# Joining the recurrence's diagonal with its last level, and asking for head norms before applying them, in a two-block kernel on one core

## The chip, the cores and the metric

The kernel runs on one core of a Trainium2 chip. The metric is the device time of one execution in microseconds (us); the median of three runs before the change is 1014.35 us (1013.6 to 1016.02).

## The reference, cut to what matters

The reference applies a first block (two layers) and a second block (two layers) to 256 tokens of 1024 channels, all in float32. The parts that the change touches are the first block's recurrence, its head norms, and a head norm in the second block's odd mixer:

```
# recurrence (per head, chunks of 64 tokens): A is lower triangular, its diagonal has decay 1
decay = exp(where(causal, b[t] - b[s], -inf))
A = einsum('bhtd,bhsd,bhtsd->bhts', qi, ki, decay)
o = einsum('bhts,bhsv->bhtv', A, vi) + einsum('bhtd,bhdv->bhtv', qi * exp(b), S)
o_hg = rmsnorm(o_hg, hgrn_onorm_g[i])
qn  = rmsnorm(heads(nq, 8), nsa_qnorm_g[i])             # 8 query heads of 64
k_sl = partial_rope(rmsnorm(heads(ksl, 2), ...), cos, sin)   # and k_wn: key heads of 64
gv = rmsnorm_2(g.reshape(..., 8, 64), g_norm)           # odd mixer, gate heads
```

## The kernel before

The 256 tokens are two halves of 128, called H = 0 and H = 1, and nearly every step is done once for each. Weights stream from memory in tiles `raw` of 128x1024; ScalarE rounds each to `whi` and VectorE subtracts to get the rest `wlo`; a projection multiplies whi by x, wlo by x and whi by the rest of x (`mm3`). The pools are small: three raw tiles, five whi and wlo, eight PSUM banks of which `pM`, `pB` and `pC` are single, `pA` two and `acc` three.

The order on each engine is made by a scheduler from the program: it takes the instructions by program order and readiness and gives buffers out as they come free, so a product of a later projection is put between dependent steps. Each engine then runs its own list in that order; an instruction that waits holds up those behind it.

The steps of a first-block layer that matter here, in program order: the key projections `K1` (PSUM `K`, 512 columns, of which the last 256 are four key heads); the projection `hi`; `hkT`, the transposed keys of the recurrence; `ph`, the first products of the compression; `hgrn` for both halves; the query projection `nq` (PSUM `Q`) and `k2` (PSUM `K`, 280 columns); the sparse attention `nsa` (`as`, `apt`, `no`); the gates `hz`, `hgo`, `nz`; and the output product `po`.

`head_rstd` (L528) squares on ScalarE (`sq`), sums on VectorE (`hss`), scales (`hv`), takes the power on GpSimd (`hr`, L412), and, where a row factor f is given, multiplies by f on VectorE (L541). For the keys and the queries it is called inside the loop over halves, right before its result is used (`kn`, `qn`).

`hgrn` (L923) builds the transposed matrix `AT` of a half. At its start four products `pd` of kT and q give every entry, and a copy under a mask of the diagonal (L936) keeps the diagonal. Then seven levels: level lv takes the decays `E`, multiplies keys and queries into them, makes four products `pl` of 128x64 and copies them into AT under that level's mask (L975). The last level, lv 6, has blocks of one token. At the end AT is multiplied with `vh` into `ho`; for H = 1 a product `ptop` and its copy `stop` carry the first half's state.

```
pd = ps_("pd", "pM")
V.copy_predicated(AT[H], lmask_d..., pd...)                       # L936, diagonal
tt(Xv[:, :, :, 0, :], Xv[:, :, :, 0, :], kv[:, :, :, 0, :], OP.mult)   # keys into E
mm(p[:, n * 64:(n + 1) * 64], X[:, n, :], Xv[:, n, :, 1, :])
V.copy_predicated(dst, lmask[:, lv]..., p...)                     # L975, one level
```

Of the kernel before, what the change touches and what calls it, by code (L numbers as in the profile page):

```python
# [14 lines left out]
AF = mybir.ActivationFunctionType  # L15
# [208 lines left out]
def body(ctx: ExitStack, tc: tile.TileContext, a: dict, offs: dict, out: bass.AP):  # L224
# [40 lines left out]
    def tt(o, x, y, op):  # L265
        V.tensor_tensor(o, x, y, op=op)  # L266
# [262 lines left out]
    def head_rstd(ps, nh, width, scale, bias, tag="t2", st="sm", f=None):  # L529

        sq = s2("sq", tag=tag)
        n = nh * width
        act(sq[:, :n], ps, AF.Square, scale=1.0 if f is None else f)
        ss = small("hss", nh, st)
        V.tensor_reduce(ss, sq[:, :n].rearrange("p (h d) -> p h d", h=nh), axis=AX, op=OP.add)
        v = small("hv", nh, st)
        V.tensor_scalar(v, ss, scale, bias, op0=OP.mult, op1=OP.add)
        r = small("hr", nh, st)
        rpow(r, v)
        if f is not None:  # L540
            V.tensor_scalar(r, r, f, None, op0=OP.mult)  # L541
        return r


# [44 lines left out]
    def first_layer(l, nx, nxt, whf=None, lb=None, between=None, whq=None, then=lambda: None):  # L589
# [82 lines left out]
        if l == 0:  # L672
            logs()
        kns = []
        for H in range(2):
            ps = pj[H]
            pk = ps[:, 256:]
            r = head_rstd(pk, 4, 64, 1.0 / 64, EPS, f=rs[H][0])
            kn = s1("kn", tag="t2")
            tt(v3(kn, 4), v3(pk, 4), bc(r, 64), OP.mult)  # L680

            kd = s2("kd", tag="t2").rearrange("p (b g a c) -> p b g a c", b=2, g=2, a=2)
            kn4 = kn.rearrange("p (b g c) -> p b g c", b=2, g=2)
            for a_ in range(2):
                tt(kd[:, :, :, a_, :], kn4, kg[:, 64:].rearrange("p (b c) -> p b c", b=2).unsqueeze(2).to_broadcast([P, 2, 2, 64]), OP.mult)
            kd8 = kd.rearrange("p b g a c -> p (b g a) c")
            rope_heads(kd8, kd8, 8, H)
            kns.append(kd.rearrange("p b g a c -> p b g (a c)"))
# [28 lines left out]
        for H in range(2):  # L717
            o = hgrn(H, lfs[H], ks[H], qT, vh, Ktop)
            r = head_rstd(o, 4, P, 16.0 / P, 16 * EPS, "pr", "sh")
            tt(v3(ys[H], 4), v3(o, 4), bc(r, P), OP.mult)  # L720


        qnT = s4("qnT").rearrange("p (j t) -> p j t", j=4)
# [6 lines left out]
        w = win("k2")  # L730
        vs, gs = [], []
        pj = proj_both(x, w, "K2", "pA")
        for H in range(2):
            ps = pq[H]
            r = head_rstd(ps, 8, 64, 1.0, 64 * EPS, f=rs[H][0])
            qn = s2("qn")
            tt(v3(qn), v3(ps), bc(r, 64), OP.mult)
            tt(v3(qn), v3(qn), bm(qg, 8), OP.mult)
            qr = s2("qr")
            act(qr, qn, AF.Copy)  # L740
            rope_heads(v3(qr), v3(qn), 8, H)
            sl = slice(H * P, (H + 1) * P)
            pt = ps_("qT", "pB")
            for j in range(4):
                PE.transpose(pt[:, j * P:(j + 1) * P], qn[:, j * P:(j + 1) * P], ident)
            V.tensor_copy(qnT[:, :, sl], pt.rearrange("p (j t) -> p j t", j=4))
            q2 = s4("q2", F32R).rearrange("p (n a c) -> p n a c", n=8, a=2)
            act(q2[:, :, 0, :], v3(qr), AF.Copy)
            tt(q2[:, :, 1, :], v3(qr), q2[:, :, 0, :], OP.subtract)
            q2 = q2.rearrange("p n a c -> p n (a c)").bitcast(F32)  # L750
            qs.append(s4("qs", F32R).rearrange("p (n t) -> p n t", n=8))
            for n0 in (0, 4):
                pt = ps_("qT", "pB")
                for n in range(4):
                    PE.transpose(pt[:, n * P:(n + 1) * P], q2[:, n0 + n, :], ident)
                p3 = pt.rearrange("p (n t) -> p n t", n=4)
                if n0:
                    V.tensor_copy(qs[H][:, n0:n0 + 4], p3)
                else:
                    act(qs[H][:, n0:n0 + 4], p3, AF.Copy)  # L760
# [163 lines left out]
    def hgrn(H, lf, kT, qT, vh, Ktop):  # L924


        lv0 = H
        near, off = slice((1 - H) * 64, (2 - H) * 64), slice(H * 64, (H + 1) * 64)
        K3 = Ktop.rearrange("p (h t) -> p h t", h=4)
        kT = kT.rearrange("p (h t) -> p h t", h=4)  # L930
        q = qT[:, :, H * P:(H + 1) * P]

        pd = ps_("pd", "pM")
        for n in range(4):
            mm(pd[:, n * P:(n + 1) * P], kT[:, n, :], q[:, n, :])
        V.copy_predicated(AT[H], lmask_d.rearrange("p (h t) -> p h t", h=4), pd.rearrange("p (h t) -> p h t", h=4))  # L936
        o = ps_("ho", "pC")
        far = small("far", 4, "sf")
        pl = tops = None
        for e4 in range(2):  # L940
            E = wk.tile([P, 4, 4, P], F32, tag="w8", name="E4", bufs=BUFS["w8"])
            for n in range(4):
                ps = ps_("D", "pA")
                for b in range(2):
                    r = (9 * b + 1 - H + 4 * e4) * 64
                    mm(ps[:, b * 256:(b + 1) * 256], lf[b][:, n * P:(n + 1) * P], lev[:, r:r + 256])
                act(E[:, :, n, :].rearrange("p v (b t) -> p b v t", b=2), ps.rearrange("p (b v t) -> p b v t", b=2, v=4), AF.Exp)
            if e4 == 0:

                V.tensor_copy(far.unsqueeze(2), E[:, 0, :, (127, 63)[H]:(128, 64)[H]])  # L950
            for e in range(4 * e4, 4 * e4 + 4):
                lv = e - lv0
                if not 0 <= lv < 7:
                    continue
                w = 64 >> lv
                X = E[:, e % 4, :, :]
                Xv = X.rearrange("p h (b u m) -> p h b u m", u=2, m=w)
                kv = kT.rearrange("p h (b u m) -> p h b u m", u=2, m=w)
                qv = q.rearrange("p h (b u m) -> p h b u m", u=2, m=w)
                tt(Xv[:, :, :, 0, :], Xv[:, :, :, 0, :], kv[:, :, :, 0, :], OP.mult)  # L960
                tt(Xv[:, :, :, 1, :], Xv[:, :, :, 1, :], qv[:, :, :, 1, :], OP.mult)
                if lv == 0:


                    if H:
                        tops = E[:, 0]
                        tt(tops[:, :, near], tops[:, :, near], q[:, :, near], OP.mult)
                    tt((tops if H else K3)[:, :, off], X[:, :, off], bc(far, 64), OP.mult)
                if lv % 2 == 0:
                    pl = ps_("pl", ("pM", "pB")[lv // 2 % 2])  # L970
                p = pl[:, lv % 2 * 256:(lv % 2 + 1) * 256]
                for n in range(4):
                    mm(p[:, n * 64:(n + 1) * 64], X[:, n, :], Xv[:, n, :, 1, :])
                dst = AT[H].rearrange("p h (b u m) -> p (h b) u m", u=2, m=w)[:, :, 1, :]
                V.copy_predicated(dst, lmask[:, lv].rearrange("p h (b m) -> p (h b) m", m=w),  # L975
                                  p.rearrange("p (b m) -> p b m", m=w))
        if H == 0:
            tt(K3[:, :, near], E[:, 3, :, near], kT[:, :, near], OP.mult)
            for n in range(4):
                mm(o[:, n * P:(n + 1) * P], AT[0][:, n, :], vh[0][:, n * P:(n + 1) * P])  # L980
        else:
            px = ps_("ptop", "pM")
            for n in range(4):
                mm(px[:, n * P:(n + 1) * P], Ktop[:, n * P:(n + 1) * P], tops[:, n, :])
            st = s2("stop", tag="pts")
            V.tensor_copy(st, px)
            for n in range(4):
                sl = slice(n * P, (n + 1) * P)
                mm(o[:, sl], AT[1][:, n, :], vh[1][:, sl], True, False)
                mm(o[:, sl], st[:, sl], vh[0][:, sl], False, True)  # L990
        return o
# [193 lines left out]
    def odd_layer(nx, nxt):  # L1185
# [88 lines left out]
                bass.AP(tensor=sap.tensor, offset=sap.offset + par * P, ap=[[0, 64], [2 * P, 4], [1, P]]))  # L1274
        w = win("g")
        pj = proj_both(x, w, "og")
        ms = []
        for H in range(2):
            g = s2("og", tag="gate")
            act(g, pj[H], AF.Gelu_apprx_tanh, scale=rs[H][0])  # L1280
            r = head_rstd(g, 8, 64, 1.0 / 64, EPS)
            tt(v3(g), v3(g), bc(r, 64), OP.mult)
            tt(g, g, sg, OP.mult)
            pm = ps_("pm", "pB")
            for n in range(8):
                mm(pm[n % 2 * 64:n % 2 * 64 + 64, n // 2 * P:(n // 2 + 1) * P], g[:, n * 64:(n + 1) * 64], ws[:, n, :])
            m = s2("mx", tag="nz")
            tt(m, pm, sb, OP.add)
            ms.append(m.rearrange("p (j t) -> p j t", j=4))
# [190 lines left out]
```

## Time and profile before

| | |
|---|---|
| median of 3 runs | 1014.35 us |
| the profiled execution | 1014.08 us |
| its span | 1012.3 us |
| TensorE busy (PE) | 982.1 us, 97% |
| VectorE busy (DVE) | 824.9 us, 81% |
| ScalarE busy (ACT) | 624.0 us, 62% |
| GpSimd busy (POOL) | 45.7 us, 5% |
| granted TensorE clock | 0.9 or more of full speed in every fortieth of the span |

The span runs from the first to the last instruction. Matmuls overlap and their ends are modelled, so PE's busy share says that PE is hardly ever without work, not that it works at its peak; the start of one matmul to the start of the next is the better measure of what one costs. A float32 product shows as two records, one for each of its two weight loads. In a row of the timeline the bracket is the idle time of that engine just before the row and what ended it.

### The profile page before, as it was taken

To read this page: it belongs to the slowest core of one execution; us is meant where nothing else is said; L and a number is where in the kernel's file an instruction comes from. 1 tells how busy PE (TensorE), PEld (TensorE's weight loads), DVE (VectorE), ACT (ScalarE), POOL (GpSimd) and SP (SyncE) were. 2 spreads that over 40 slices of the span, in tenths; PEclk is the share of its full clock that TensorE was granted. 3 is DMA by queue.
4 is the path that set the end of the run, shared out by engine and by line. 5 is a ranking of instruction groups with operands and counts; after the bars stand their busy time and mean duration, and the time that the engine had idled before them with its cause. 6 is when DMAs were issued, how large, how long until landed. Compare 5 with 4: busy or idle time off the path is not lost.

```text
span 1012.3 us, 16208 instructions
## 1 busy us (share of the span) xinstructions
PE 982.1 (97%) x6009; PEld 841.3 (83%) x6009; DVE 824.9 (81%) x1482; ACT 624.0 (62%) x1128; POOL 45.7 (5%) x52
## 2 busy tenths in 40 slices
PE   9999999999998999999999999999999999999997
PEld 6889786788797876799889888888898889888885
DVE  5878899878788898779879988888677889888886
ACT  7753565577644664666657666666756457666664
POOL 1001100000002000000111000000000020000000
PEclk9999999999999999999999999999999999999999
DMA  8832533664504526555754766666572546766661
GB/s 320 304 104 74 181 114 109 215 194 137 182 11 129 164 63 184 170 158 165 231 185 132 223 195 189 191 192 181 167 226 66 169 127 198 215 187 188 187 188 62
DMA packets 49103, 169.02 MB, mean 167 GB/s; under 512 B 5760, under 2 KB 7040, under 8 KB 48384
## 3 DMA queue, kind: packets, MB, share of 16 engines
q1 hardware_dynamic: 48448, 167.17, 54.1%
q8 instruction: 47, 0.77, 0.3%
q10 hardware_dynamic: 576, 0.82, 0.2%
q14 instruction: 32, 0.26, 0.1%
HBM read 165.34 MB, written 1.05 MB: 164 GB/s over the span
## 4 chain that ended last, share of the span: by engine, by line
PE 64%; DVE 9%; ACT 4%; DMA 4%; issue 2%; POOL 1%; POOLq 0%; ACTq 0%; DVEq 0%; SPq 0%
PE up L365 25%; PE pd L365 11%; PE po L365 5%; PE pg L365 3%; DVE wlo L266 3%; PE oq L365 2%; ACT whi L263 2%; PE as L365 1%; PE xT L431 1%; PE xa L365 1%; PE pl L365 1%; PE nz L365 1%; PE hgo L365 1%; PE og L365 1%; PE Q L365 1%
## 5 line engine op out<-in xcount | busy, mean ns | idle before, releaser
L266 DVE TENSOR_TENSOR wlo<-raw,whi 128x1024 fp32r<-128x1024 f32 (+2 forms) x297 | 358.6, 1211 | 86.7 <-ACT whi L263 86.1
L263 ACT ACTIVATE whi<-raw 128x1024 fp32r<-128x1024 f32 (+2 forms) x297 | 309.6, 1045 | 164.8 <-DMA raw<-in_win_dram 17.8
L365 PE MATMUL up<-xN,whi 128*128 128x512 f32 x512 | 180.8, 397 | 0.0
L365 PE MATMUL up<-xN,wlo 128*128 128x256 f32 x512 | 133.3, 281 | 0.0
L365 PE MATMUL pd<-whi,fhl 128*128 128x512 f32 x352 | 115.4, 391 | 0.1
L365 PEld LDWEIGHTS up<-xN,whi 128*128 128x128 f32 x512 | 94.1, 188 | 18.6
L365 PEld LDWEIGHTS up<-xN,wlo 128*128 128x128 f32 x512 | 96.6, 189 | 5.7
L1073 DVE SCALAR_TENSOR_TENSOR fc<-fp,colp,fc 128x255 f32<-128x255 f32 (+1 forms) x176 | 81.5, 479 | 3.0 <-ACT fc L263 0.7
L365 PEld LDWEIGHTS pd<-whi,fhl 128*128 128x128 f32 x352 | 66.0, 188 | 13.0 <-ACT fhl L263 0.5
L365 PE MATMUL pd<-wlo,fhl 128*128 128x512 f32 x176 | 68.6, 390 | 0.0
L263 ACT ACTIVATE upl<-up 128x256 f32<-128x256 f32 x64 | 24.5, 383 | 59.4 <-PE up L365 59.3
L263 ACT ACTIVATE fc<-fp,colp 128x256 f32<-128x256 f32 x88 | 51.0, 590 | 3.9 <-DVE fp L266 3.8
L365 PE MATMUL po<-whi,yA 128*128 128x512 f32 x128 | 41.5, 399 | 2.4 <-ACT yA L263 1.3
L263 ACT ACTIVATE pr<-as,anm 128x128 f32<-128x128 f32 (+1 forms) x80 | 32.5, 422 | 17.8 <-PE apt L1056 6.8
L365 PE MATMUL pg<-whi,xB 128*128 128x512 f32 x128 | 40.6, 393 | 0.0
L365 PEld LDWEIGHTS pd<-wlo,fhl 128*128 128x128 f32 x176 | 33.1, 188 | 6.9
L365 PE MATMUL up<-xD,whi 128*128 128x256 f32 x192 | 35.2, 284 | 0.9 <-DVE xD L436 0.6
L365 PE MATMUL up<-xF,whi 128*128 128x256 f32 x192 | 35.2, 284 | 0.9 <-DVE xF L436 0.6
L266 DVE TENSOR_TENSOR fp<-up,upl 128x256 f32<-128x256 f32 x64 | 27.0, 421 | 10.7 <-ACT upl L263 10.5
L365 PE MATMUL K<-whi,xA 128*128 128x280 f32 (+1 forms) x128 | 33.8, 345 | 0.0
L263 ACT ACTIVATE jk<-h 128x512 f32<-128x512 f32 x36 | 22.7, 637 | 17.4 <-DVE h L266 17.4
L412 POOL TENSOR_TENSOR r<-v,mh 128x2 f32<-128x2 f32 (+1 forms) x10 | 6.7, 672 | 582.0 <-DVE v L472 196.5
(397 smaller groups left out, 2272.6 us busy)
## 6 DMA issues: line engine op xcount, KB each, us to landing
raw<-in_up_dram SPq DMA_DIRECT2D x88, 512.0 KB, 3.6
raw<-in_win_dram SPq DMA_DIRECT2D x62, 512.0 KB, 4.3
raw<-in_down_dram SPq DMA_DIRECT2D x44, 512.0 KB, 3.7
raw<-in_ein_dram SPq DMA_DIRECT2D x20, 512.0 KB, 4.0
raw<-in_oin_dram SPq DMA_DIRECT2D x20, 512.0 KB, 3.8
raw<-in_wout_dram SPq DMA_DIRECT2D x16, 512.0 KB, 3.7
raw<-in_wpg_dram SPq DMA_DIRECT2D x16, 512.0 KB, 4.0
cw<-in_cw_dram SPq DMA_DIRECT2D x4, 1024.0 KB, 7.8
```

What stands on the lines that cost most here:

```text
L263: A.activation(o, i, f, **kw)
L266: V.tensor_tensor(o, x, y, op=op)
L365: PE.matmul(o, l, r, start=start, stop=stop)
L412: G.tensor_tensor(o, v, mh[:, :v.shape[1]], op=OP.pow)
L431: PE.transpose(ps[:, j * P:(j + 1) * P], hc[:, j * P:(j + 1) * P], ident)
L1073: V.scalar_tensor_tensor(dst[:, k:], src[:, :T - k], w, dst[:, k:], op0=OP.mult, op1=OP.add)
```

## The change

It has three parts. First, `head_rstd` no longer multiplies by f; its callers give f to a `scalar_tensor_tensor` that applies f and the norm to the data at once. Second, the norms of both halves are asked for (square, sum, power) ahead of the loop that applies them: for the keys (K1), the queries (nq) and the gate of the odd mixer (og); and the second half's `y` from the recurrence's norm is applied inside the query loop. Third, in `hgrn` the four products `pd` at the start and their copy are gone. At the last level q is copied by ScalarE beside the decayed queries, and one product of 256 columns per head, with kT itself as weights, gives the diagonal (z = 0) and the last level (z = 1); the decay of the last level's even tokens is 1, so the keys need no multiplication. The results lie in banks pB and pM, two heads each, and go to AT by two masked copies per bank: 256 columns under the diagonal's mask and the 128 odd ones under the level's.

```diff
@@ head_rstd
         rpow(r, v)
-        if f is not None:
-            V.tensor_scalar(r, r, f, None, op0=OP.mult)
         return r
@@ first_layer, K1
+        krs = [head_rstd(pj[H][:, 256:], 4, 64, 1.0 / 64, EPS, f=rs[H][0]) for H in range(2)]
         for H in range(2):
-            ps = pj[H]
-            pk = ps[:, 256:]
-            r = head_rstd(pk, 4, 64, 1.0 / 64, EPS, f=rs[H][0])
+            pk = pj[H][:, 256:]
             kn = s1("kn", tag="t2")
-            tt(v3(kn, 4), v3(pk, 4), bc(r, 64), OP.mult)
+            V.scalar_tensor_tensor(v3(kn, 4), v3(pk, 4), rs[H][0], bc(krs[H], 64), op0=OP.mult, op1=OP.mult)
@@ first_layer, after hgrn
-            tt(v3(ys[H], 4), v3(o, 4), bc(r, P), OP.mult)
+            if H == 0:
+                tt(v3(ys[H], 4), v3(o, 4), bc(r, P), OP.mult)
@@ first_layer, queries
+        qrs = [head_rstd(pq[H], 8, 64, 1.0, 64 * EPS, f=rs[H][0]) for H in range(2)]
         for H in range(2):
-            ps = pq[H]
-            r = head_rstd(ps, 8, 64, 1.0, 64 * EPS, f=rs[H][0])
             qn = s2("qn")
-            tt(v3(qn), v3(ps), bc(r, 64), OP.mult)
+            V.scalar_tensor_tensor(v3(qn), v3(pq[H]), rs[H][0], bc(qrs[H], 64), op0=OP.mult, op1=OP.mult)
             tt(v3(qn), v3(qn), bm(qg, 8), OP.mult)
+            if H == 0:
+                tt(v3(ys[1], 4), v3(o, 4), bc(r, P), OP.mult)
@@ hgrn
-        pd = ps_("pd", "pM")
-        for n in range(4):
-            mm(pd[:, n * P:(n + 1) * P], kT[:, n, :], q[:, n, :])
-        V.copy_predicated(AT[H], lmask_d.rearrange("p (h t) -> p h t", h=4), pd.rearrange("p (h t) -> p h t", h=4))
@@ hgrn, level loop
+                tt(Xv[:, :, :, 1, :], Xv[:, :, :, 1, :], qv[:, :, :, 1, :], OP.mult)
+                if lv == 6:
+                    z = E[:, 0, :, :]
+                    act(z, q, AF.Copy)
+                    for i in range(2):
+                        pl = ps_("pl", ("pB", "pM")[i]).rearrange("p (n z t) -> p n z t", n=2, z=2)
+                        for n in range(2):
+                            mm(pl[:, n], kT[:, 2 * i + n, :], E[:, 0:e % 4 + 1:e % 4, 2 * i + n, :])
+                        hs = slice(2 * i, 2 * i + 2)
+                        dst = AT[H][:, hs]
+                        V.copy_predicated(dst, lmask_d.rearrange("p (h t) -> p h t", h=4)[:, hs], pl[:, :, 0])
+                        odd = lambda t: t.rearrange("p h (b u) -> p h b u", u=2)[:, :, :, 1]
+                        V.copy_predicated(odd(dst), lmask[:, lv, hs], odd(pl[:, :, 1]))
+                    continue
                 tt(Xv[:, :, :, 0, :], Xv[:, :, :, 0, :], kv[:, :, :, 0, :], OP.mult)
-                tt(Xv[:, :, :, 1, :], Xv[:, :, :, 1, :], qv[:, :, :, 1, :], OP.mult)
@@ odd_layer, gate
+            ogs.append((g, head_rstd(g, 8, 64, 1.0 / 64, EPS)))
+        for g, r in ogs:
             tt(v3(g), v3(g), bc(r, 64), OP.mult)
```

The scheduler makes another order of it in the two layers of the first block. On every engine the rows behind them, with the odd mixer's gate among them, stand as before but for buffer numbers.

VectorE at the key norms of the first layer before (`K_408` and `K_409` are the two halves of K1's PSUM, `hr` the norm, `kn` the normed keys, `blk` the compression's blocks):

```order
L537 TENSOR_SCALAR hv<-hss 128x4
L541 TENSOR_SCALAR hr<-hr,r 128x4
L266 TENSOR_TENSOR kn<-K_408,hr 128x256
L266 TENSOR_TENSOR wlo<-raw,whi 128x1024
L266 TENSOR_TENSOR blk<-kvp,colp 128x16x15
...
L535 TENSOR_REDUCE hss<-sq 128x4
L266 TENSOR_TENSOR kd<-rA,rB 128x8x16
...
L266 TENSOR_TENSOR kn<-K_409,hr 128x256
```

And the same place of the change:

```order
L537 TENSOR_SCALAR hv<-hss 128x4
L266 TENSOR_TENSOR blk<-kvp,colp 128x16x15
L266 TENSOR_TENSOR wlo<-raw,whi 128x1024
...
L266 TENSOR_TENSOR blk<-kvp,colp 128x16x15 x2
L535 TENSOR_REDUCE hss<-sq 128x4
L677 SCALAR_TENSOR_TENSOR kn<-K_408,r,hr 128x256
L537 TENSOR_SCALAR hv<-hss 128x4
...
L677 SCALAR_TENSOR_TENSOR kn<-K_409,r,hr 128x256
```

The multiplication by f is gone, two weight splits and four blocks stand ahead of the first `kn`, and the second half's sum stands before it. On PE the second half of `hi`, whose PSUM bank the first `kn` frees, starts after 23 of the first half's 24 products, where it started after three.

VectorE at the query norms of the first layer before (`Q_969` is the first half's PSUM; `he` and `hT` belong to the compression):

```order
L537 TENSOR_SCALAR hv<-hss 128x8
L266 TENSOR_TENSOR wlo<-raw,whi 128x1024
L891 RECIPROCAL he<-he 128x32
L541 TENSOR_SCALAR hr<-hr,r 128x8
L266 TENSOR_TENSOR hT<-ph,he 128x32
L266 TENSOR_TENSOR qn<-Q_969,hr 128x512
L535 TENSOR_REDUCE hss<-sq 128x4
```

And of the change (`Q_962` is the first half, `AT_89` the second half's matrix):

```order
L537 TENSOR_SCALAR hv<-hss 128x8
L266 TENSOR_TENSOR wlo<-raw,whi 128x1024
L966 COPY_PREDICATED AT_89<-lmaskd,pl 128x256 x2
L968 COPY_PREDICATED AT_89<-lmask,pl 128x128 x2
L535 TENSOR_REDUCE hss<-sq 128x8
L734 SCALAR_TENSOR_TENSOR qn<-Q_962,r,hr 128x512
L995 COPY stop<-ptop 128x512
L889 TENSOR_SCALAR he<-he 128x32
...
L266 TENSOR_TENSOR qn<-qn,rowp 128x512
L890 RECIPROCAL he<-he 128x32
L266 TENSOR_TENSOR rA<-qn,colp 128x128
L266 TENSOR_TENSOR hT<-ph,he 128x32
```

Between `hv` and `qn` there are now the four masked copies of the recurrence's end and the second half's sum; a multiplication and a part of the rotation stand ahead of `hT`, where a split and the multiplication by f stood.

PE at the end of the second half's recurrence in the first layer of the change (`pl` with `hkT` is the joined product, `K_1044` and `K_1045` the two halves of k2):

```order
L365 MATMUL pl<-E_863 128x64 x4
L365 MATMUL pl<-E_863,hkT 128x256 x4
L365 MATMUL K_1045<-whi,xA_108 128x280
L365 MATMUL K_1044<-whi,xA_108 128x280
...
L365 MATMUL ho<-vh,AT_89 128x128
L365 MATMUL ptop<-E_820,Ktop 128x128 x4
L365 MATMUL ph<-colp,hq_669 128x32
```

Ten products of k2 lie between the joined product and `ho`, and `ptop` now stands behind the first `ho`; before, `ptop` stood ahead of it and seven products of k2 behind the last level.

## Rows read from the trace of the kernel before

**Rows 1.** Sums by stage: window, length, then busy time (instructions) of each engine

```profile
core 0: us, PE busy (x) PEld busy (x) DVE busy (x) ACT busy (x) POOL busy (x), PEclk, DMA share, GB/s
62.00:92.00 30.00, 29.99 (x243) 27.10 (x239) 23.54 (x64) 13.77 (x24) 1.01 (x1) 1.00 0.11 34
92.00:112.00 20.00, 17.38 (x121) 15.46 (x121) 15.91 (x39) 9.49 (x15) 6.01 (x3) 1.00 0.44 132
```

**Rows 2.** Timeline of PE, first layer: start, length, instruction, [idle before <-what ended it]

```profile
45.95 0.50 PE L365 MATMUL hi<-whi,xA 128*128 128x512 f32 x1 [0.94 <-DVE kn L266]
46.29 0.39 PE L365 MATMUL hi<-wlo,xA 128*128 128x512 f32 x1
46.52 0.62 PE L365 MATMUL hi<-whi,xA 128*128 128x512 f32 x2
...
60.95 1.08 PE L365 MATMUL ph<-cw,blk 128*32 128x128 f32 x32 [0.81 <-DVE hkT L703]
...
98.03 0.41 PE L365 MATMUL ph<-colp,hq 128*128 128x32 f32 x2 [0.74 <-DVE hT L266]
...
105.89 0.63 PE L755 MATMUL qT<-ident,q 128*128 128x128 f32 x4 [0.52 <-DVE hv L537]
...
110.88 0.63 PE L745 MATMUL qT<-ident,qn 128*128 128x128 f32 x4 [1.36 <-DVE qn L266]
...
170.71 0.50 PE L365 MATMUL po<-whi,yA 128*128 128x512 f32 x1 [1.34 <-ACT yA L263]
```

**Rows 3.** Timeline of PE, the same places of the second layer

```profile
273.79 1.08 PE L365 MATMUL ph<-cw,blk 128*32 128x128 f32 x32 [0.50 <-DVE hkT L703]
...
310.87 0.41 PE L365 MATMUL ph<-colp,hq 128*128 128x32 f32 x2 [0.63 <-DVE hT L266]
...
318.80 0.63 PE L755 MATMUL qT<-ident,q 128*128 128x128 f32 x4 [0.70 <-DVE hv L537]
...
323.85 0.63 PE L745 MATMUL qT<-ident,qn 128*128 128x128 f32 x4 [1.44 <-DVE qn L266]
...
381.79 0.73 PE L365 MATMUL po<-whi,yA 128*128 128x512 f32 x2 [1.04 <-DVE yA L409]
```

**Rows 4.** Timeline of DVE, key norms of the first layer

```profile
45.14 0.23 DVE L541 TENSOR_SCALAR hr<-hr,r 128x4 f32<-128x4 f32 x1 [1.13 <-POOL hr L412]
45.47 0.42 DVE L266 TENSOR_TENSOR kn<-K,hr 128x256 f32<-128x256 f32 x1
45.81 1.22 DVE L266 TENSOR_TENSOR wlo<-raw,whi 128x1024 fp32r<-128x1024 f32 x1
...
48.40 1.03 DVE L266 TENSOR_TENSOR blk<-kvp,colp 128x240 f32<-128x240 f32 x3
```

**Rows 5.** Timeline of DVE, query norms of the first layer

```profile
97.66 0.23 DVE L541 TENSOR_SCALAR hr<-hr,r 128x8 f32<-128x8 f32 x1 [1.26 <-POOL hr L412]
...
108.56 0.23 DVE L541 TENSOR_SCALAR hr<-hr,r 128x8 f32<-128x8 f32 x1 [1.53 <-POOL hr L412]
```

**Rows 6.** Timeline of PE: diagonal, two levels, a 256-column float32 product, each with its successor

```profile
58.16 1.06 PE L365 MATMUL pd<-hqT,hkT 128*128 128x128 f32 x8
58.98 0.70 PE L365 MATMUL Q<-whi,xA 128*128 128x512 f32 x2
...
90.26 1.89 PE L365 MATMUL pl<-E 128*128 128x64 f32 x16
91.96 0.38 PE L365 MATMUL K<-whi,xA 128*128 128x280 f32 x1
...
455.82 1.94 PE L365 MATMUL lg<-xc,bd 128*128 128x256 f32 x8
457.40 0.47 PE L365 MATMUL bp<-xC,wlo 128*128 128x256 f32 x1
```

**Rows 7.** Groups by form: count | busy us, mean ns of one | idle before

```profile
L975 DVE COPY_PREDICATED AT<-lmask,pl 128x256 f32<-128x256 uint8 x28 | 14.6, 523 | 8.4 <-PE pl L365 8.1
L936 DVE COPY_PREDICATED AT<-lmaskd,pd 128x512 f32<-128x512 uint8 x4 | 2.9, 736 | 0.0
...
L263 ACT ACTIVATE qr<-qn 128x512 f32<-128x512 f32 x4 | 2.5, 632 | 4.8 <-DVE qn L266 4.4 <-DVE hv L537 0.2
```

More of the change, by code (lines that the diff above doesn't have):

```diff
@@ L1276, in odd_layer @@
         pj = proj_both(x, w, "og")
-        ms = []
+        ms, ogs = [], []
         for H in range(2):
@@ L1280, in odd_layer @@
             act(g, pj[H], AF.Gelu_apprx_tanh, scale=rs[H][0])
-            r = head_rstd(g, 8, 64, 1.0 / 64, EPS)
+            ogs.append((g, head_rstd(g, 8, 64, 1.0 / 64, EPS)))
+        for g, r in ogs:
             tt(v3(g), v3(g), bc(r, 64), OP.mult)
```

## Prediction

> **What bounds the kernel now.** I read the page's first part first: PE is busy for 97% of the span, so the time is the sum of PE's work and of the few moments in which it waits. Then the sums by stage show where those moments lie [rows 1]: in the recurrence (62 to 92 us) PE is busy 29.99 of 30 us, since products of the query projection fill the steps of the levels; in the 20 us behind it only 17.38. The timeline of PE names each wait: 0.94, 0.81, 0.74, 0.52, 1.36 and 1.34 us in the first layer [rows 2], 0.50, 0.63, 0.70, 1.44 and 1.04 us at the same places of the second [rows 3]. What ends them is nearly always VectorE, which runs its list in order. Its own rows show why it is late: at the key norms it stands idle for 1.13 us until GpSimd's power comes back, and only then multiplies by f and normalizes [rows 4]; at the query norms it stands idle for 1.26 and 1.53 us in the same way [rows 5]. So a part of PE's waits is GpSimd's power, passed on by VectorE's order.
>
> **The change part by part.**
>
> *The joined product.* PE loses the diagonal's eight records, 0.82 us from 58.16 to 58.98, and the last level's eight, half of the 1.70 us from 90.26 to 91.96, or 0.85 [rows 6]: 1.67 us for each half. It gains eight records of 256 columns. The trace has that form elsewhere: eight float32 records of 256 columns took 1.58 us from 455.82 to 457.40 [rows 6]. So 0.09 us for each half come off, 0.4 over two halves and two layers; but in the first half the order breaks the joined product into three pieces, and each break costs a weight load that nothing hides, at most the 0.11 us of one 64-column record (1.70 by 16). I take 0 for PE, with -0.4 and +0.4 as ends. VectorE loses a copy of 512 columns (0.74), one of 256 (0.52 as a mean) and a multiplication (0.42, the size of `kn` [rows 4]), and gains two copies of 256 and two of 128, each of the latter between 0.23 (the smallest operation, rows 4) and 0.52 [rows 7]: 1.68 against 1.50 to 2.08, so about even. ScalarE gains a copy of 512 columns, 0.63 [rows 7], in a stretch where it is busy 13.77 of 30 us [rows 1]: covered. In the first half it has the three products and the two of a decay between level 4 and the joined product; if that cover is gone, PE waits up to 0.63 us, once per half.
>
> *The key norms.* In the first layer PE's wait of 0.94 us is for the first `kn`, which frees a PSUM bank for the second half of `hi` [rows 2]. Now the first half's products are put first. At the wait's start (45.0 us) three of them are done; 20 more at 0.23 (46.29 to 46.52, rows 2) keep PE until 49.6. The first `kn` moves back: two splits of 1.22, four blocks of 0.34 (1.03 by three) and the second half's sum (taken as 0.42, like `kn`) now stand ahead, less the idle 1.13 and the multiplication of 0.23 [rows 4]: 45.89 + 2.44 + 1.37 + 0.42 - 1.36 = 48.8. It is 0.8 us early, so the whole 0.94 goes. Late next is the split of the last `hi` weights, which now has to be there for the first half alone; it is the second of the two splits, some 1.2 us ahead of `kn`, and is needed six products before the end (48.2), so 0.6 us of cover. In the second layer there is no such wait.
>
> *The first compression product* (0.81 and 0.50) waits for a copy of `hkT` behind weight splits [rows 2, 3]. VectorE reaches those splits about 1.4 us sooner, by the second half's idle time and multiplication at the key norms (taken like the first's). But PE also comes sooner, by the 0.94 of the first layer, while four products of the queries stand where `pd` stood. I take 0.8 of the 1.31 as gone; ends 0 and 1.31.
>
> *The second compression product* (0.74 and 0.63) waits for `hT`. Ahead of `hT` a split of 1.22 and an idle 1.26 with its 0.23 stood; now a multiplication of 512 columns (below 0.74, the copy of that size) and a small rotation (0.3). All of the 1.37 goes; end: nothing of it.
>
> *The first half's queries* (0.52 and 0.70): this wait I expect to grow. PE arrives without the wait just named and with products of k2 already spent as filler in the recurrence, whereas VectorE still has to normalize the second half of `y`, whose power is asked for late, and two splits of 1.22 stand there. I take 1.0 us in each layer, +0.8 in all; ends 0 and 2.4 each (two splits).
>
> *The second half's queries* (1.36 and 1.44): their power was asked for behind the first half's rotation and took 1.53 idle us [rows 5]; now it is asked for before the first `qn`, long ahead. All of the 2.80 goes; end: half of it.
>
> *The output product* (1.34 and 1.04) waits for `yA`, on ScalarE behind the last softmax exponentials in the first layer and on VectorE in the second [rows 2, 3]. With both halves' queries ready sooner the attention ends sooner and the last score blocks lie in the gates instead of in `po`. I take half, 1.2; ends 0 and 2.38.
>
> *The odd mixer's gate* keeps its order on every engine: 0.
>
> *New waits.* Some 300 rows of PE in each layer stand in another order, and the eleven waits of rows 2 and 3 have a mean of 0.91 us. I add one in each layer, 2.0 in all.
>
> The sum: -0.94 - 0.8 - 1.37 + 0.8 - 2.80 - 1.2 + 2.0 + 0 = -4.3 us. Against the profiled execution's own 1014.08 (span 1012.3 and 1.8 around it) that is 1009.8; this execution lies 0.27 under the median, so 1010.0.
>
> **The rivals.**
>
> *The waits only move.* VectorE does as much as before, and PE's waits come where its list and VectorE's cross. For it: VectorE's work is even, as worked out, and one of the terms already grows. Against it: 5.3 idle us of VectorE behind GpSimd go (1.13, 1.26 and 1.53 in rows 4 and 5, and the second half's keys), and that idle time lay right ahead of PE's waits. It gives 1013 to 1015.
>
> *Slower: VectorE's in-order list at the end of the recurrence.* The copies into `AT` now come last: four of them, behind a split of the next weights, and `ptop` needs bank pM, so it cannot start before the last copy, where it ran beside it. PE has ten products of 280 columns between, 1.3 us at 0.13. Of the copies 2 x 0.52 + 2 x 0.4 = 1.8 and the split's 1.22 make 3.0, of which the joined product's second piece (0.8) hides another part: PE then waits 0.9 us if the split starts on time. It decides as soon as that split itself is late, because its weights are: late by three splits (3.7 us) it makes PE wait 4.6 us in each layer, +9 in all, and with -4.3 for the rest the time is 1019. Against it: transfers rest in that stage (DMA share 0.11, rows 1), so the weights should lie ready.
>
> *The joined product costs its weight loads alone.* Records of 64 and 128 columns cost the same, 0.11 and 0.10 us [rows 6]; if 256 columns cost no more, eight records take 0.85 and 0.8 us come off each half, 3.3 in all: 1006.7. Against it is the 1.58 us of the same form [rows 6].
> The Trainium skill (TensorE: Matmul & The Clock Gate, Back-to-back issue gap and LDWEIGHTS) gives N/2.4 + 2.5 ns for a lone matmul, 109 ns for 256 columns, beside 107 ns for a load of 128 columns. By that rule the eight records would take 0.87 us; the trace's 0.20 us a record contradicts it for float32.
>
> *All terms, no new waits*: -6.3, or 1008; with the full ends of the compression's, the queries' and the output's terms -8.8, or 1005.5.
>
> **How the numbers follow.** The forecast, 1007.5 to 1012.5, has 0.50; the waits only move 0.24; slower at the recurrence's end 0.14; the weight loads alone 0.05; everything gained 0.07. No change means within 0.2%, 2.0 us, about what a measurement of this kernel can tell: 1012.3 to 1016.4. Faster takes nearly all of the forecast (0.48), the last two (0.12) and a few of the moved waits (0.04): 0.64. Same takes most of the moved waits and the forecast's edge, 0.22. Slower keeps 0.14. The range from 1006.5 to 1015 leaves out the slow rival and a little below.
>
> **What would show it.** Each wait of rows 2 and 3 has its place in the new profile: no idle time ahead of `hi` and of the second `qn`'s transposes; about 1 us ahead of the first half's `qT`; idle time of VectorE behind GpSimd only at `y`. The joined product should take about 1.6 us a half. I am wrong if PE waits at `ptop` or `ho` for copies into `AT`, if a row of `hi` waits for its last split, or if PE's busy time itself changes by more than 0.5 us.

## The result, and the profile after

The changed kernel takes 1003.88 us (median of 4 runs, 1002.23 to 1005.38) against 1015.06 (4 runs, 1013.6 to 1016.02): a ratio of 0.989, 95% interval 0.9869 to 0.991. The forecast was 1010.0 with 1006.5 as the lower end, so the time lies below the range. The profiled execution, 1005.38 us, is the slowest of the four; its span is 1003.6 us, 8.7 under that of [rows 1].

The sums of the two stages (columns as in rows 1) show where it went. In the 20 us behind the recurrence PE was busy 17.38 [rows 1]; now it is 19.81:

```profile
62.00:92.00 30.00, 29.89 (x205) 26.53 (x202) 24.40 (x65) 14.17 (x25) 1.75 (x2) 1.00 0.19 59
92.00:112.00 20.00, 19.81 (x130) 17.28 (x129) 18.83 (x43) 10.98 (x17) 4.68 (x3) 1.00 0.46 132
```

PE's timeline of the first layer, at the places of [rows 2]:

```profile
42.79 0.69 PE L365 MATMUL kvp<-colp,kv 128*64 128x64 f32 x16 [0.23 <-ACT kv L263]
...
59.09 1.08 PE L365 MATMUL ph<-cw,blk 128*32 128x128 f32 x32
...
97.50 0.31 PE L365 MATMUL ph<-colp,hq 128*128 128x32 f32 x2
...
101.35 0.66 PE L744 MATMUL qT<-ident,qn 128*128 128x128 f32 x4 [0.19 <-DVE hv L266]
...
103.77 0.63 PE L754 MATMUL qT<-ident,q 128*128 128x128 f32 x4
...
107.02 0.60 PE L744 MATMUL qT<-ident,qn 128*128 128x128 f32 x4
...
159.95 0.50 PE L365 MATMUL pp<-wlo,pxh 128*128 128x512 f32 x1 [0.37 <-DVE wlo L266]
...
167.74 0.50 PE L365 MATMUL po<-whi,yA 128*128 128x512 f32 x1 [0.34 <-ACT yA L263]
```

A row without a bracket shows no wait of 0.15 us or more: both compression products, the first half's `q` and the second half's `qn` come without one. The output product keeps 0.34 of 1.34. New are 0.23, 0.19 and 0.37. The second layer reads the same: of [rows 3] only `po` keeps 0.34, and 0.18, 0.37 and 0.04 more at `kvp` are new.

VectorE shows why. At the key norms it no longer stands still [rows 4]: between `hv`, whose power GpSimd takes, and the first `kn` lie 3.8 us of other work.

```profile
44.88 0.17 DVE L537 TENSOR_SCALAR hv<-hss 128x4 f32<-128x4 f32 x1
44.96 0.40 DVE L266 TENSOR_TENSOR blk<-kvp,colp 128x240 f32<-128x240 f32 x1
45.27 1.22 DVE L266 TENSOR_TENSOR wlo<-raw,whi 128x1024 fp32r<-128x1024 f32 x1
...
46.72 1.22 DVE L266 TENSOR_TENSOR wlo<-raw,whi 128x1024 fp32r<-128x1024 f32 x1
...
48.49 0.41 DVE L535 TENSOR_REDUCE hss<-sq 128x4 f32<-128x256 f32 x1
48.81 0.48 DVE L677 SCALAR_TENSOR_TENSOR kn<-K,r,hr 128x256 f32<-128x256 f32 x1
```

At the query norms the 1.26 and 1.53 of [rows 5] are gone, and the only row that waits for a power is `y`:

```profile
91.00 0.20 DVE L537 TENSOR_SCALAR hv<-hss 128x8 f32<-128x8 f32 x1
91.04 1.22 DVE L266 TENSOR_TENSOR wlo<-raw,whi 128x1024 fp32r<-128x1024 f32 x1
92.17 0.78 DVE L966 COPY_PREDICATED AT<-lmaskd,pl 128x256 f32<-128x256 uint8 x2
92.84 0.73 DVE L968 COPY_PREDICATED AT<-lmask,pl 128x128 f32<-128x128 uint8 x2
93.37 0.65 DVE L535 TENSOR_REDUCE hss<-sq 128x8 f32<-128x512 f32 x1
93.93 0.75 DVE L734 SCALAR_TENSOR_TENSOR qn<-Q,r,hr 128x512 f32<-128x512 f32 x1
...
100.51 0.69 DVE L266 TENSOR_TENSOR y<-ho,hr 128x512 f32<-128x512 f32 x1 [0.86 <-POOL hr L412]
...
102.94 0.68 DVE L266 TENSOR_TENSOR q<-qr,q 128x512 fp32r<-128x512 f32 x1
```

The joined product took 1.76 us from 90.27 to 92.03, 0.09 more than the 1.67 worked out for what it replaces [rows 6]:

```profile
90.27 2.11 PE L365 MATMUL pl<-E,hkT 128*128 128x256 f32 x8
92.03 0.61 PE L365 MATMUL K<-whi,xA 128*128 128x280 f32 x2
```

### The profile page after: what moved, and what is told of

Same layout as the page of the kernel before. It is cut to its first block, busy times and chain, and to the rows that moved or that the text cites. A ratio compares the mean times of both kernels' runs of the same rounds, so it can differ in the third digit from the quotient of the medians.

```text
span 1003.6 us, 16146 instructions
## 1 busy us (share of the span) xinstructions
PE 981.6 (98%) x5977; PEld 839.2 (84%) x5977; DVE 822.1 (82%) x1478; ACT 627.3 (63%) x1132; POOL 45.5 (5%) x52
## 4 chain that ended last, share of the span: by engine, by line
PE 80%; DVE 7%; ACT 5%; DMA 4%; issue 2%; POOL 1%; POOLq 0%; SPq 0%; ACTq 0%; DVEq 0%
PE up L365 25%; PE pd L365 11%; PE po L365 7%; PE pg L365 4%; PE pl L365 3%; DVE wlo L266 3%; PE nz L365 2%; PE Q L365 2%; PE hi L365 2%; PE as L365 2%; PE hgo L365 2%; ACT whi L263 2%; PE oq L365 2%; DMA raw<-in_win_dram 2%; PE no L365 1%
```

## The experiments

My theory after the result: the gain is GpSimd's power no longer standing between VectorE and PE, and the joined product is nearly neutral. Rivals: the joined product brings most, or the parts work only together.

### The parts alone

e1, the norms' part whole, with the recurrence of before:

```diff
- r = head_rstd(pk, ..., f=rs[H][0])        # in the loop, and r *= f in head_rstd
+ krs = [head_rstd(pj[H][:, 256:], ..., f=rs[H][0]) for H in range(2)]   # ahead; queries alike
```


> The norms' part alone (both halves' powers asked for first, f folded into the normalization); the recurrence keeps its separate diagonal and last level. Theory 1 (the whole gain is GpSimd's power no longer standing between VectorE and TensorE, and the joined product costs TensorE 0.2 us a half): 10 to 12 us faster than before, 1002.5 to 1004.5, with the waits at the compression and at both halves' queries gone as in the changed kernel. Theory 2 (the joined product brings most): 2 to 5 us faster, 1009.5 to 1012.5. Theory 3 (the parts only work together, through the order of the fill): 4 to 8 us faster, and the sum of this run and the next is short of 11 us by 3 or more.

Measured: 1008.76 us, ratio 0.9942 (0.9925 to 0.9959), 5.9 us faster.

e2, the joined product, with the norms of before:

```diff
- pd = ...; V.copy_predicated(AT[H], lmask_d, pd)
+ if lv == 6: ... mm(pl[:, n], kT[:, 2 * i + n, :], E[:, 0:e % 4 + 1:e % 4, 2 * i + n, :])
```


> The joined product alone; the norms as before, multiplied by f and asked for one after the other. Theory 1: 0 to 1.5 us slower than before (TensorE's 22.98 us for diagonal and last level become 19.98 against 3.31 fewer, some 0.85 us more or less), 1014.5 to 1016. Theory 2: 6 to 9 us faster, 1006 to 1009. Theory 3: within 1 us of before.

Measured: 1011.34 us, ratio 0.996 (0.9945 to 0.9974), 3.3 us faster. Neither number is that of my theory: the norms' part brings half, and the product, which costs PE no less, gains by itself. Added they give 9.2 of the 11.2 us, so at this level little needs both parts together.

e3, only the fold:

```diff
- V.tensor_scalar(r, r, f, None, op0=OP.mult)          # in head_rstd
- tt(v3(qn), v3(ps), bc(r, 64), OP.mult)
+ V.scalar_tensor_tensor(v3(qn), v3(ps), rs[H][0], bc(r, 64), op0=OP.mult, op1=OP.mult)   # kn alike
```


> Of the norms' part only the fold: no multiplication of 0.23 us by f between GpSimd's power and the normalization; the powers are still asked for one half after the other. If the saved VectorE steps were the cause: half of the gain or more, 1005 to 1009. Theory 1, in which it is the idle time behind GpSimd: two steps of 0.23 us stand ahead of each pair of waits, four in each layer, so 1 to 2.5 us faster, 1012.5 to 1014.

Measured: 1019.02 us, ratio 1.0045 (1.0031 to 1.0058): 4.4 us slower, though VectorE has eight instructions fewer. VectorE's idle time at GpSimd is as before, now in front of `kn` and `qn`, and PE waits at three places where the kernel before waited less (0, 0 and 1.04 us). Why the scheduler's order makes these waits no run shows. First VectorE, then PE of e3:

```profile
45.67 0.48 DVE L678 SCALAR_TENSOR_TENSOR kn<-K,r,hr 128x256 f32<-128x256 f32 x1 [1.14 <-POOL hr L412]
...
97.82 0.75 DVE L735 SCALAR_TENSOR_TENSOR qn<-Q,r,hr 128x512 f32<-128x512 f32 x1 [1.26 <-POOL hr L412]
...
108.58 0.75 DVE L735 SCALAR_TENSOR_TENSOR qn<-Q,r,hr 128x512 f32<-128x512 f32 x1 [1.53 <-POOL hr L412]
```

```profile
127.58 0.74 PE L365 MATMUL as<-kA,qs 128*128 128x256 f32 x4 [1.59 <-ACT g L263]
...
192.91 0.66 PE L431 MATMUL xT<-ident,h 128*128 128x128 f32 x4 [1.70 <-DVE h L266]
...
406.04 1.26 PE L431 MATMUL xT<-ident,h 128*128 128x128 f32 x8 [2.11 <-DVE h L266]
```

e4, the fold, and the keys' powers alone asked for first:

```diff
+ krs = [head_rstd(...) for H in range(2)]      # keys; the queries stay in the loop
```


> The fold, and the keys' powers of both halves asked for ahead of both normalizations; the queries' still one after the other. Theory 1: the key norms' wait (0.94) and the first compression product's (0.81 and 0.50) go, the second half's queries keep their 1.36 and 1.44: 4 to 6 us faster than before, 1009 to 1011, so about 3 us below the fold alone. If the queries' powers bring nearly all: within 1 us of the fold alone.

Measured: 1016.86 us, ratio 1.0017 (1.0001 to 1.0032). PE's waits at `hi` and at the first `ph` are gone in both layers, as expected, but it is 2.2 us under the fold alone, not 3 or more, and not under the kernel before.

### Each edit with and without the others

e5 asks first but keeps the multiplication by f; e6 is the changed kernel with it put back; e7 is the joined product and the fold, asked in the loop.

```diff
  rpow(r, v)
+ if f is not None:                              # e5 on e1, e6 on the changed kernel
+     V.tensor_scalar(r, r, f, None, op0=OP.mult)
```


> Both halves' powers asked for ahead of the normalizations (and the second half's y moved), but the multiplication by f is kept, and the recurrence is as before: the same instructions as before in another order. Additive theory (each edit has its own price wherever it stands: the fold +4.4 us, asking first 1008.8 less 1019.0 = -10.3): 1003.5 to 1006. Order theory (the fold's +4.4 is the price of one particular list, not of the instructions): 1006 to 1011, near the 1008.8 of the norms' part whole. If the 0.23 us multiplications behind GpSimd matter by themselves here: 1 to 2 us above 1008.8, since they stand between GpSimd and the normalizations.

> The changed kernel with the multiplication by f put back behind each power of keys and queries (eight of 0.16 to 0.23 us on VectorE). Additive theory: 4 us faster than the changed kernel, 999 to 1001. Order theory: within 2 us of the changed kernel's 1003.9, 1002 to 1006, slower rather than faster because VectorE does 1.8 us more.

> The joined product and the fold, but the powers of the second half asked for inside the loop as before. Additive theory: the product's -3.3 and the fold's +4.4, 1014.5 to 1017. Order theory: no such sum; 1008 to 1013, with the second half's queries still waiting 1.2 us in each layer and the key norms 1.4 us in the first.

Measured: e5 1011.97 us, ratio 0.9969 (0.9957 to 0.998); e6 1011.39, 0.9967 (0.9955 to 0.9979); e7 1010.62, 0.9954 (0.994 to 0.9969). All eight combinations (medians in us; those of before were 1014.35 to 1015.42):

| | f multiplied, asked in loop | f folded, asked in loop | f multiplied, asked first | f folded, asked first |
|---|---|---|---|---|
| diagonal first | 1014.65 | 1019.02 | 1011.97 | 1008.76 |
| joined product | 1011.34 | 1010.62 | 1011.39 | 1003.88 |

None of these edits has a price of its own. The fold costs 4.4 us alone and gains 7.5 beside the other two; asking first gains nothing on the joined product while f is multiplied, and 6.7 once it is folded. VectorE's rows of e5 show the link:

```profile
44.76 0.17 DVE L537 TENSOR_SCALAR hv<-hss 128x4 f32<-128x4 f32 x1
46.06 0.23 DVE L541 TENSOR_SCALAR hr<-hr,r 128x4 f32<-128x4 f32 x1 [1.13 <-POOL hr L412]
...
97.98 0.23 DVE L541 TENSOR_SCALAR hr<-hr,r 128x8 f32<-128x8 f32 x1 [1.27 <-POOL hr L412]
...
101.50 0.23 DVE L541 TENSOR_SCALAR hr<-hr,r 128x8 f32<-128x8 f32 x1 [1.52 <-POOL hr L412]
```

The multiplication is the first reader of the power, and the list puts it where the power is asked for: VectorE stands still although `kn` and `qn` come later. This standing goes only if nothing reads the power until it is used. Asking first is not worthless without that: e5 is 2.7 us faster than the kernel before, and PE no longer waits at the second half's `qn`, since VectorE's standing for the second power (1.52) has moved ahead of the first `qn`. There PE now waits 0.98 us; the second row is the second half:

```profile
103.81 0.66 PE L746 MATMUL qT<-ident,qn 128*128 128x128 f32 x4 [0.98 <-DVE qn L266]
...
110.81 0.66 PE L746 MATMUL qT<-ident,qn 128*128 128x128 f32 x4
```

e9 and e10 test the first reader: f is still multiplied, but by GpSimd behind its own power; e9 stands on e5, e10 on e6.

```diff
- V.tensor_scalar(r, r, f, None, op0=OP.mult)
+ G.tensor_tensor(r, r, f.to_broadcast([P, nh]), op=OP.mult)
```


> As the run in which both powers are asked first and f is still multiplied (1011.97), but the multiplication by f is done by GpSimd behind its own power, so that no VectorE instruction reads the power before the normalization itself. Theory by place (VectorE's list puts the first reader of a power right behind the request, and stands there for GpSimd; only where the first reader is the normalization, which itself stands later, is that time used): near the norms' part whole, 1007.5 to 1010, and no idle time of VectorE behind GpSimd of about 1.1 us at the key norms. Theory by work (the eight multiplications of 0.23 us themselves, now slower on GpSimd): no better than 1011 to 1013.

> The same with the joined product: the changed kernel with f multiplied on GpSimd behind each power. Theory by place: 1003 to 1006, against 1011.39 with the multiplication on VectorE. Theory by work: 1010 to 1013.

Measured: e9 1009.78 us, ratio 0.9947 (0.9928 to 0.9965), beside e1's 1008.76; e10 1005.37, 0.9907 (0.9887 to 0.9927), beside the changed kernel's 1003.88 and e6's 1011.39. The multiplication is still done, but no longer as VectorE's first reader of the power. e10 is the clear case: its interval lies apart from that of e6, and over the first block its VectorE list is that of the changed kernel, row for row (the normalization is a plain multiplication there). The eight multiplications that VectorE is spared are 1.8 us at most (0.23 each), not the 6.0 between e6 and e10; the rest goes with the standing and with the list, which is another one in e6. No run parts these two. The intervals of e9 and e5 overlap. In e9 VectorE's wait at the first `kn` is gone and 0.25 us stands at the second (0.80 at the first `qn`):

```profile
48.43 0.41 DVE L266 TENSOR_TENSOR kn<-K,hr 128x256 f32<-128x256 f32 x1
...
50.48 0.42 DVE L266 TENSOR_TENSOR kn<-K,hr 128x256 f32<-128x256 f32 x1 [0.25 <-POOL hr L541]
```

e8, the changed kernel with the second half's y in its old place:

```diff
-             if H == 0:
-                 tt(v3(ys[H], 4), ...)
+             tt(v3(ys[H], 4), v3(o, 4), bc(r, P), OP.mult)
```


> The changed kernel with the second half's y applied where it stood in the program before, right behind its power, instead of in the query loop. If the place of y freed the first half's queries (their 0.52 and 0.70 us wait went where I forecast 1.0 each): those waits come back, 1.2 us or more, 1005 to 1007. If the queries came sooner because their rotation no longer stands behind y (the power is back by the recurrence's end) and y's place is set by GpSimd anyway: within 1 us of 1003.9, same order on VectorE around y.

Measured: 1004.23 us, ratio 0.9889 (0.9873 to 0.9906). Over the first block VectorE's and PE's lists are those of the changed kernel, row for row: the scheduler puts `y` at the same place, and VectorE still waits 0.87 us for its power. So moving `y` in the program did nothing; another place in the list was not tried.

### What the joined product does

e11 keeps it at the end but splits it:

```diff
- mm(pl[:, n], kT[:, 2 * i + n, :], E[:, 0:e % 4 + 1:e % 4, 2 * i + n, :])
+ for zz in range(2):
+     mm(pl[:, n, zz], kT[:, 2 * i + n, :], E[:, zz * (e % 4), 2 * i + n, :])
```


> The changed kernel with the joined product of 256 columns split into a product of 128 columns for the diagonal and one of 128 for the last level, both still at the recurrence's end (sixteen records a half instead of eight). If the join itself saves TensorE time: 16 records at 0.10 to 0.11 us are 1.7 us against 1.79 measured for eight of 256 columns, so no saving, and 1003 to 1005 here. If the gain of the recurrence's part came from fewer records (sixteen before, eight now): its 4.9 us come back, 1007 to 1009.

Measured: 1005.16 us, ratio 0.9898 (0.9882 to 0.9915). The join itself is worth little: the intervals overlap, VectorE's list over the first block is that of the changed kernel, and from start to start PE's records of it come to 7.70 us in 64 against 7.15 in 32. The product's 4.9 us (1008.76 less 1003.88) must then come from the rest of the part: the diagonal at the end, no multiplication of the last level's keys, four smaller copies in place of two. No run takes these one by one; that it is the diagonal's place is argued from what is seen at two places. The four masked copies and a split lie between `hv` and the first `qn`: in e2 VectorE's idle time at that power is 0.21 us, against 1.26 [rows 5], without any change of the norms:

```profile
93.09 0.20 DVE L537 TENSOR_SCALAR hv<-hss 128x8 f32<-128x8 f32 x1
93.13 1.22 DVE L266 TENSOR_TENSOR wlo<-raw,whi 128x1024 fp32r<-128x1024 f32 x1
94.27 0.78 DVE L967 COPY_PREDICATED AT<-lmaskd,pl 128x256 f32<-128x256 uint8 x2
94.94 0.73 DVE L969 COPY_PREDICATED AT<-lmask,pl 128x128 f32<-128x128 uint8 x2
95.88 0.23 DVE L541 TENSOR_SCALAR hr<-hr,r 128x8 f32<-128x8 f32 x1 [0.21 <-POOL hr L412]
```

And the order at the layer's end is another one. In e1 PE waits there for the residual `h`, which on VectorE stands behind a split of weights that came late from memory; in the changed kernel it does not. SP's queue, second layer, of e1 and then of the changed kernel:

```profile
381.82 8.34 SPq L258 DMA_DIRECT2D raw<-in_wout_dram  x4
391.17 7.53 SPq L258 DMA_DIRECT2D raw<-in_wpg_dram  x4
```

```profile
380.10 3.18 SPq L258 DMA_DIRECT2D raw<-in_wout_dram  x2
...
384.86 0.34 SPq L258 DMA_DIRECT2D raw<-in_wpg_dram  x1
```

The last weights of the output product are asked for by 383.3 instead of 390.2 (start and length added), the next ones (`wpg`) 6.3 us sooner, and the wait of 1.58 us that e1 has at `xT` (at 396.67, second layer) is absent. Why the list comes out so was not tried: no run here changes the layer's end alone.

### GpSimd's power, twice

e12 is the kernel before, e13 the changed kernel, each with every head norm's power done twice.

```diff
  rpow(r, v)
+ rpow(r, v)
```


> The kernel before with each head norm's power on GpSimd done twice (the second writes the same values), some 1.0 us more for 128x4 and 1.0 to 2.5 for 128x8. If VectorE's standing behind the power is passed on to TensorE: the key norms of the first layer (one wait of 0.94), the compression and both halves' queries grow by about 1 us each in each layer, 6 to 12 us slower than before, 1021 to 1027. If TensorE's waits come from elsewhere in VectorE's list: within 3 us of before.

> The changed kernel with each head norm's power on GpSimd done twice, as in the run that cost the kernel before 15.6 us. Theory by place: the powers of keys and queries now lie beside other VectorE work (2.7 us between the end of the first key power and its use), so most of the doubling is covered; what stays exposed are the second half's y and the places where the list had only 0.2 us to spare: 3 to 8 us slower than the changed kernel, 1007 to 1012. If the changed kernel gained elsewhere and still stands behind GpSimd as before: 13 us or more slower, 1017 and above.

Measured: e12 1031.0 us, ratio 1.0167 (1.0146 to 1.0189), 15.6 us slower than before; e13 1018.9 us, ratio 1.004 (1.0021 to 1.006) to before, 15.0 above the changed kernel. The first says that GpSimd's latency is on the path. The second is not what I expected: the changed kernel pays as much. Its VectorE rows in the first layer:

```profile
53.35 0.48 DVE L678 SCALAR_TENSOR_TENSOR kn<-K,r,hr 128x256 f32<-128x256 f32 x1 [1.05 <-POOL hr L412]
...
99.18 0.75 DVE L735 SCALAR_TENSOR_TENSOR qn<-Q,r,hr 128x512 f32<-128x512 f32 x1 [1.48 <-POOL hr L412]
107.45 0.69 DVE L266 TENSOR_TENSOR y<-ho,hr 128x512 f32<-128x512 f32 x1 [1.89 <-POOL hr L412]
```

The first `kn` and the second `qn` take the doubling without a wait; the second `kn`, the first `qn` and `y` do not. Over both layers VectorE's idle time behind the powers of keys and queries rises by 4.6 us (from 0), against 11.0 in e12 (from 9.2), so more than half of that doubling is covered. The waits at `y`, which the change does not remove, rise by 4.2 and 4.5. They reach PE: `q`, which stands behind `y` in VectorE's list, makes it wait 1.15 us in the first layer. The order moved as well: the idle times of PE's rows sum to 25.3 us over the whole span, against 15.1 in the changed kernel and 23.2 before. So the 15.0 us do not tell how much of the latency the change covered, and how they divide between `y`, the two exposed powers and the order stays open.

## Why the prediction was wrong

The mechanism held in most places: no idle time of VectorE behind the powers of keys and queries, no `hi`, compression or second-half wait, nothing at `ptop` or `ho`, PE's busy time 981.6 against 982.1 us, just at the bound of 0.5. Two signs failed: no 1 us stands ahead of the first half's `qT`, and VectorE waits behind GpSimd not only at `y` but also for 0.66 us in each layer at `kc`, the compression's keys. The sum failed too: -4.3 against -8.7 us between the two profiled executions. Term by term, from the timelines of both layers (a pitch is the time from the start of one record to the start of the next):

| term | forecast | measured |
|---|---|---|
| joined product | 0 | +0.85 (pitches: 7.15 us in 32 records, against 3.31 for `pd` and 2.99 for the level) |
| key norms (`hi`) | -0.94 | -0.94 |
| first compression product | -0.8 | -1.31 |
| second compression product | -1.37 | -1.37 |
| first half's queries | +0.8 | -0.85 (1.22 gone, 0.37 new at the `qn` ahead) |
| second half's queries | -2.80 | -2.80 |
| output product | -1.2 | -1.70 |
| `xT` of `h` behind it | not in the sum | -1.3 (0.29 and 1.04 gone) |
| new waits | +2.0 | +1.2 (`kvp` 0.27, `pp` 0.74, `pl` 0.20 in waits of 0.10) |

The measured waits sum to -9.1 of idle time; other idle time differs at the span's start (+0.9), at `apt` (-0.2) and behind the first block (+0.2). PE's busy time fell by 0.5 although the joined product costs 0.85 more. That product was priced at 1.58 a half and took 1.79; what it replaces was priced at 1.67 and had taken 1.58 by its pitches.

The step that failed is "the first half's queries: this wait I expect to grow", with "whereas VectorE still has to normalize the second half of `y`, whose power is asked for late, and two splits of 1.22 stand there". `y` does come late and waits 0.86 us. What I left out is the queue ahead of it: `qn` starts at 93.93 (97.92 before), so its rotation and the second half's sum stand ahead of `y`, where before they stood behind it; `q` is done at 103.6 instead of 105.7, 2.1 us sooner, and PE arrives 1.6 us sooner. I had counted PE's gain and not VectorE's at the same place. That is 1.65 of the 4.4 us: forecast +0.8, measured -0.85. The end that I gave this wait, 0, would have been a term of -1.22; the sum of full ends, -8.8, took it as unchanged instead. With -1.22 it is -10.0, or 1004.3.

Second, the allowance of 2.0 us for new waits was 0.8 too large, and it had no counterpart: waits that I had not read can go as well, and those of `xT`, at 202.39 and 400.70 in the kernel before, went (1.3). Third, two terms had the right sign and were taken in the middle (`ph`, `po`); they came at or near their full end, 1.0 in all. These are 4.8 us too little in gain, less the 0.85 of the joined product. The 0.5 that is then left of 4.4 is a balance outside the terms: PE's other rows were busy 1.35 us less, other idle time grew by 0.9; no run says why. The rival "all terms" with its full ends gave 1005.5 with a chance of 0.07 shared with its milder form; the profiled execution took 1005.38. That is luck: it had 0 for the joined product, the first half's queries, the new waits and `xT`, which measured +0.85, -0.85, +1.2 and -1.3 and so nearly cancel. The other 2.5 us between -8.7 and the -11.2 of the medians is which executions were profiled: before's lay 1.0 under its median, after's 1.5 above.

The experiments also correct the reasons. I priced the parts as if they added up. But the key norms' wait goes in full only if both powers are asked first and VectorE reads none of them early (it is 1.37 us in e3 and 0.72 in e5), while the second queries' goes with asking first alone (e5), and the terms of the second compression product and the first half's queries also go with the joined product alone (e2), as do `po` and `xT`, for which PE there waits 1.16 us in each layer at a score block. Against the rival that the waits only move I had set 5.3 idle us of VectorE; over both layers 9.2 behind these powers went, and waits behind GpSimd at `y` and `kc` took back 3.0. The slower rival did not come, nor the 0.9 us that it had even with a split on time: PE waits at neither `ptop` nor `ho`. The split ahead of the copies started at 91.04, 0.99 before the joined product's end where 0.8 was allowed, and the four copies took 1.40 us, not 1.8; they end at 93.57, and PE reaches `ptop` at 93.72.

## What to carry to other kernels

Where an engine with an in-order list waits for a slow helper, look for the first instruction that reads the helper's result, however small: asking sooner gained little here while that reader stood at the asking (2.7 us, or nothing with the joined product), and deleting the reader gained little or lost while the next one stood there too (0.7 gained, or 4.4 lost). When a wait ahead of an engine goes, everything behind it on that engine moves forward as well: compare arrivals on both sides of the next wait before saying that it grows. Edits whose order a scheduler makes are not to be added: here the same one, the fold, was worth between +4.4 and -7.5 us.

## What was not expected of the hardware

GpSimd's multiplication of 128x4 numbers in e9 took 0.80 us beside a VectorE split and 0.20 us while VectorE stood still:

```profile
44.26 1.02 POOL L412 TENSOR_TENSOR hr<-hv,mh 128x4 f32<-128x4 f32 x1 [24.06 <-DVE hv L537]
44.89 1.22 DVE L266 TENSOR_TENSOR wlo<-raw,whi 128x1024 fp32r<-128x1024 f32 x1
...
45.36 0.80 POOL L541 TENSOR_TENSOR hr<-hr,r 128x4 f32<-128x4 f32 x1
...
50.25 0.20 POOL L541 TENSOR_TENSOR hr<-hr,r 128x4 f32<-128x4 f32 x1
```

The multiplication at 45.36 ends at 46.16, the split beside it at 46.11. The Trainium skill (SBUF — State Buffer, SBUF: two separate sides) says that a VectorE operation with two SBUF inputs and a GpSimd operation that reads SBUF shut each other out until the first is done. The multiplication agrees with it. The power ahead of it does not: the split starts while the power (44.26 to 45.28) is still running, and takes its usual 1.22 us. GpSimd's spans are rough, so this one row is a hint and no more.

The masked copies of 128 columns (every second one) were not cheaper than those of 256: 457 and 446 ns as means of eight, in the changed kernel:

```profile
L966 DVE COPY_PREDICATED AT<-lmaskd,pl 128x256 f32<-128x256 uint8 x8 | 3.3, 446 | 0.2
L968 DVE COPY_PREDICATED AT<-lmask,pl 128x128 f32<-128x128 uint8 x8 | 3.2, 457 | 0.1
```
